# One split of normed rows in the opening of a hybrid encoder layer, with column sums and forget gate from raw rows

## The chip, the cores and the metric

The kernel runs on one core of a Trainium2 chip. The metric is the device time of one execution, in microseconds (us). A core has five engines that run side by side, each through its own instructions in order: TensorE (PE, matrix products; PEld are its weight loads), VectorE (DVE), ScalarE (ACT), GpSimd (POOL) and SyncE (SP, which here issues DMAs). An engine waits for another only through semaphores.

## What is computed

One layer of an encoder trunk for 528 tokens (16 learned meta tokens and 512 of the input) and 1024 channels. The part that matters here, shortened:

```python
h = concatenate([meta, x])                       # 528 x 1024
u = h * rsqrt(mean(h*h) + 1e-6) * norm_mix       # RMSNorm
proj = u @ w_in                                  # projections for everything that follows
# of proj: wd, ad, gd (256 columns), shifted by one token and mixed with mu:
w_log = -softplus(-(w0 + tanh(wd) @ w_lora_up)) - 0.5
a = sigmoid(a0 + ad @ a_lora_up)
g = sigmoid(gd) @ g_lora_up
# of proj: fl, 8 columns, the forget gate of the attention heads
log_f = log_sigmoid(fl + b_f);  F = cumsum(log_f)
# recurrence (RWKV-7) and forgetting attention, gates, output projection,
# second RMSNorm and a squared-ReLU MLP follow
```

## The kernel before

Tokens lie along the free dimension: the input is held transposed, as 8 blocks of 128 channels by 528 tokens, in two halves of 264 tokens (`xt[0]`, `xt[1]`), each loaded in four pieces of two blocks. An fp32 product is replaced by three faster ones: both operands are split into a high and a low part of type fp32r (`uhi`, `ulo` for the input, `whi`, `wlo` for the weights), and high*high, high*low and low*high are added up in PSUM (`passes`). A high part is a cast on ACT, a low part a subtraction on DVE.

The opening (lines 333 to 401) works so. For each half and piece, ACT squares the rows (`sq`, L352). ACT and DVE make `uhi` and `ulo` from rows that are multiplied with the channel gain but not yet normed (L355, L356). PE adds the squares over the channels with a 128x128 matrix of ones in fp32 (`pss`, L360), and computes the 8 forget gate columns as split products (`pf`, L365). ACT makes the scale factor of each token, `rs`, with Ln and Exp (L368, L369). PE multiplies the first weight block (`B_LORA`: `wd` and `ad`) with the half (L304); its result is multiplied with `rs` afterwards (`normed_shift`, L377), then shifted and mixed (`tshift`, L317, L318). After both halves come the forget gate's bias, log-sigmoid and running sum (L381 to L388), tanh and split of the first block (L390, L391), and the second weight block (`B_GD`: `gd`, L393). Meanwhile DVE multiplies the rows with gain and `rs` in place (L398), and ACT and DVE split them a second time, now as normed rows (L400, L401). All later projections read this second split.

The rest of the layer is written as streams that a planner (`Turns`, `Clock`) interleaves by due times; it fixes PE's order by hand (`manual_schedule`), while the order on the other engines is the compiler's. The first things in it are the small products of the decay (`pup`, L720), which read the tanh of the first block (`lhi`, `llo`), and the projection blocks (L501), for which weights are converted at L470 (ACT) and L471 (DVE). The attention reads the forget gate's running sum `fF` through DRAM (L599). SP's queue issues the input's first half, the first weight block, the second half, the second weight block, constants, and then the weights of later blocks as buffers come free.

Of the kernel before, what the change touches and what calls it, by code (L numbers as in the profile page):

```python
# [9 lines left out]
F32 = mybir.dt.float32  # L10
# [9 lines left out]
T = 528  # L20
# [166 lines left out]
def kernel(ctx, tc, ht, x, win, par, cst, gain, lora, wout, wo, wup, wdn, out, dbg=None):  # L187
# [92 lines left out]
    with ExitStack() as st:  # L280
# [3 lines left out]
        opening = ["pj", "pj", "ch", "py"]  # L284

# [10 lines left out]
        def proj(blk, evac, parts=((0, HT), (HT, T)), w=None):  # L296

            w = w or load_w(win[blk], (G, V))
            for a0, a1 in parts:
                po = ppj(opening.pop(0))[:, :a1 - a0]  # L300
                n = 0
                for k in range(KB):
                    for a, b in passes(wk(w, k), U):
                        mm(po, a, b[:, k, a0:a1], start=n == 0, stop=n == 23)  # L304
                        n += 1
                evac(po, slice(a0, a1))

# [3 lines left out]
        def tshift(blk, dst):  # L311

            tm = rp.tile([128, 1 + T], F32, name="tm")
# [13 lines left out]
        fF = rp.tile([8, T], F32, name="fF", tag="lc")  # L327
        fF_d = dr.tile([8, T], F32, name="fF_d")
        f0 = rp.tile([8, T], F32, name="f0", tag="tha")
        f1 = rp.tile([8, T], F32, name="f1", tag="sq")  # L330
        lfs = [rp.tile([128, TP], F32, name=f"lf{i}", tag=("okk", "orr")[i]) for i in range(2)]
        lf, gf = (x[:, :T] for x in lfs)
        with tc.tile_pool(name="xp", bufs=2) as xp:
# [6 lines left out]
            w_lora = load_w(win[B_LORA])  # L340
            for c in range(4):
                nc.sync.dma_start(xt[1][:, 2 * c:2 * c + 2, :].rearrange("p a b -> p (a b)"), ht[1, c])
            w_gd = load_w(win[B_GD])
            nc.sync.dma_start(cs, cst)
            wf = [xp.tile([128, 64], F32R, name=f"wf{i}", bufs=1) for i in range(2)]
            split(wf[0], wf[1], pr[:, C_FL:])
            rss = []
            for t in range(2):
                tk = slice(HT * t, HT * t + HT)
                for c in range(4):  # L350
                    sq = xp.tile([128, 2, HT], F32, name="sq", bufs=3)
                    act(sq, xt[t][:, 2 * c:2 * c + 2, :], AF.Square)  # L352
                    for k in range(2 * c, 2 * c + 2):
                        gn = pr[:, C_GN + k:C_GN + k + 1]
                        act(uhi[:, k, tk], xt[t][:, k, :], AF.Copy, scale=gn)  # L355
                        V.scalar_tensor_tensor(ulo[:, k, tk], xt[t][:, k, :], gn, uhi[:, k, tk].bitcast(F32), ALU.mult, ALU.subtract)  # L356
                    if c == 0:
                        pq = psm("pss")[:, :HT]
                    for k in range(2):
                        mm(pq, ones, sq[:, k, :], start=c + k == 0, stop=c + k == 4)  # L360
# [1025 lines left out]
```

## Time and profile before

| what | us |
|---|---|
| median of 3 runs | 854.1 (852.3 to 855.1) |
| the profiled execution | 852.0 |
| its span, first to last instruction | 850.2 |
| PE busy in the span | 827.5 |
| first L360 product on PE | 5.66 |
| first L304 product (first weight block) | 14.45 |
| first L501 product (planned part) | 34.13 |

The times in the views count from the start of the span. The chain of waits follows the work that ended last backwards from the end; its shares say which engine's work or waits fill the time. A row of a timeline gives start, length, engine, line, operation and, in brackets, the idle time ahead of it and what ended it. The table of groups by form gives for each kind of instruction the number, the busy time, the mean length in ns, and the idle time ahead of it.

### The profile page before, as it was taken

How to read it: one execution, taken by the hardware profiler on the slowest of the kernel's cores; microseconds unless marked ns; L12 is line 12 of the kernel's file. 1: busy time of each engine (PE TensorE's matmuls, PEld its weight loads, DVE VectorE, ACT ScalarE, POOL GpSimd, SP SyncE). 2: the span in 40 equal slices, each digit the busy share in tenths (PEclk: the TensorE clock that was granted, in tenths of full speed). 3: DMA queues.
4: the chain of work that ended last, by engine and by line, in shares of the span. 5: the costliest groups of instructions: out<-in, count | busy, mean ns of one | idle time of the engine just before them, and what ended most of it. 6: DMA issues, size and time to landing. Idle time of an engine off the chain costs nothing.

```text
span 850.2 us, 15285 instructions
## 1 busy us (share of the span) xinstructions
PE 827.5 (97%) x5740; PEld 679.1 (80%) x5740; DVE 618.1 (73%) x1222; ACT 454.0 (53%) x923; POOL 133.5 (16%) x133
## 2 busy tenths in 40 slices
PE   7999989999999999999999999999999999999998
PEld 6888977878887787677788779888888888888886
DVE  6996976679867876566357564877787677768788
ACT  7857536765656337654465442664355435534452
POOL 1041300003012000000012101203700560055000
PEclk9999999999999999999999999999999999999999
DMA  6132231111222212123386432651743274346421
GB/s 225 52 103 59 64 122 43 39 55 36 71 93 82 80 58 89 39 87 100 120 286 221 151 103 75 195 165 50 240 157 99 78 250 132 87 130 192 119 93 74
DMA packets 51338, 95.88 MB, mean 113 GB/s; under 512 B 5816, under 2 KB 6968, under 8 KB 51264
## 3 DMA queue, kind: packets, MB, share of 16 engines
q1 hardware_dynamic: 47680, 86.52, 32.0%
q0 software_dynamic: 1280, 4.20, 1.6%
q10 hardware_dynamic: 2304, 4.20, 1.5%
q8 instruction: 45, 0.74, 0.4%
q14 instruction: 29, 0.24, 0.1%
HBM read 88.57 MB, written 6.31 MB: 112 GB/s over the span
## 4 chain that ended last, share of the span: by engine, by line
PE 78%; DVE 10%; DMA 5%; ACT 3%; issue 3%; POOL 1%; SPq 0%; DVEq 0%; ACTq 0%; POOLq 0%
PE pj L501 24%; PE po L1137 21%; PE po L1255 12%; PE pd L1255 5%; DMA gl<-gd 2%; PE po L1107 2%; PE psc L611 1%; PE pw L845 1%; DVE wlo L471 1%; DMA wraw<-in_wo 1%; PE py L656 1%; PE ppt L640 1%; DVE wlo L236 1%; PE psr L794 1%; PE pch L905 1%
## 5 line engine op out<-in xcount | busy, mean ns | idle before, releaser
L501 PE MATMUL pj<-uhi,whi 128*128 128x264 f32 (+1 forms) x480 | 165.9, 346 | 0.0
L501 PE MATMUL pj<-ulo,whi 128*128 128x264 f32 (+1 forms) x480 | 154.3, 321 | 1.4 <-DVE ulo L401 1.4
L501 PE MATMUL pj<-uhi,wlo 128*128 128x264 f32 (+1 forms) x480 | 154.3, 321 | 0.0
L501 PEld LDWEIGHTS pj<-uhi,whi 128*128 128x128 f32 x480 | 90.3, 188 | 15.0 <-issue 6.7
L236 DVE TENSOR_TENSOR wlo<-wraw,whi 128x512 fp32r<-128x512 f32 x88 | 70.4, 809 | 38.2 <-ACT whi L235 35.9
L501 PEld LDWEIGHTS pj<-ulo,whi 128*128 128x128 f32 x480 | 90.6, 189 | 8.2 <-issue 1.7
L501 PEld LDWEIGHTS pj<-uhi,wlo 128*128 128x128 f32 x480 | 90.4, 188 | 7.2
L1137 PE MATMUL po<-zhi,whi 128*128 128x512 f32 (+1 forms) x248 | 94.8, 382 | 0.0
L1137 PE MATMUL po<-zlo,whi 128*128 128x512 f32 (+1 forms) x248 | 94.8, 382 | 0.0
L1137 PE MATMUL po<-zhi,wlo 128*128 128x512 f32 (+1 forms) x248 | 94.8, 382 | 0.0
L235 ACT CAST whi<-wraw 128x512 fp32r<-128x512 f32 x88 | 53.8, 617 | 51.4 <-DMA wraw<-in_wup 23.3
L471 DVE TENSOR_TENSOR wlo<-wraw,whi 128x512 fp32r<-128x512 f32 x80 | 61.3, 773 | 17.3 <-ACT whi L470 16.9
L470 ACT CAST whi<-wraw 128x512 fp32r<-128x512 f32 x80 | 48.9, 617 | 35.1 <-PE pj L501 33.8
L270 ACT CAST whi<-t 128x512 fp32r<-128x512 f32 x64 | 39.9, 624 | 44.4 <-DVE wlo L271 20.6
L271 DVE TENSOR_TENSOR wlo<-t,whi 128x512 fp32r<-128x512 f32 x64 | 49.3, 782 | 18.9 <-ACT whi L270 18.0
L1255 PE MATMUL po<-wlo,fhi 128*128 128x512 f32 x160 | 62.7, 392 | 0.2 <-DVE wlo L271 0.2
L1255 PE MATMUL po<-whi,flo 128*128 128x512 f32 x160 | 62.3, 390 | 0.0
L1255 PE MATMUL po<-whi,fhi 128*128 128x512 f32 x160 | 61.9, 389 | 0.0
L1183 POOL TENSOR_TENSOR t<-traw 128x512 f32<-128x512 f32 x24 | 34.9, 1462 | 155.1 <-DVE wlo L271 136.0
L1137 PEld LDWEIGHTS po<-zlo,whi 128*128 128x128 f32 x248 | 46.6, 188 | 9.1
L1137 PEld LDWEIGHTS po<-zhi,wlo 128*128 128x128 f32 x248 | 46.6, 188 | 9.0
L1137 PEld LDWEIGHTS po<-zhi,whi 128*128 128x128 f32 x248 | 46.6, 188 | 9.0
(307 smaller groups left out, 1754.8 us busy)
## 6 DMA issues: line engine op xcount, KB each, us to landing
wraw<-in_win SPq DMA_DIRECT2D x84, 256.0 KB, 2.6
wraw<-in_wup SPq DMA_DIRECT2D x64, 256.0 KB, 3.4
wraw<-in_wdn SPq DMA_DIRECT2D x48, 256.0 KB, 2.7
traw<-in_wdn SPq DMA_DIRECT2D x48, 256.0 KB, 3.0
gd<-gt ACTq DMA_DIRECT2D x16, 256.0 KB, 2.2
wraw<-in_wout SPq DMA_DIRECT2D x16, 256.0 KB, 3.1
gl<-gd SPq DMA_DIRECT2D x16, 256.0 KB, 3.2
wraw<-in_wo SPq DMA_DIRECT2D x16, 256.0 KB, 3.5
```

Source lines behind the costliest of these rows:

```text
L235: A.copy(hi, raw)
L236: low.tensor_tensor(lo, raw, hi.bitcast(F32), ALU.subtract)
L270: A.copy(hi, x)
L271: V.tensor_tensor(lo, x, hi.bitcast(F32), ALU.subtract)
L470: A.copy(hi, raw)
L471: low.tensor_tensor(lo, raw, hi.bitcast(F32), ALU.subtract)
L501: mm(po, a, b[:, k, a0:a1], start=n == 0, stop=n == 23)
L611: mm(sc, q[hs, 128 * i:128 * i + 128], k[hs, a:b], start=True, stop=True)
L1107: mm(po, a[:, k, 128 * i:128 * i + 128], b[:, k, :], start=n == 0, stop=n == 23)
L1137: mm(po[:, t0:t1], a, b[:, k, t0:t1], start=n == 0, stop=n == 23)
L1183: eng.tensor_tensor(t, sums[c, pair] if c in (T1, T2) else c, d, ALU.add)
L1255: mm(x[i], a[:, k, left, 128 * i:128 * i + 128], c, start=start and k == 0 and n == 0, stop=stop and k == n_pairs - 1 and n == 2)
```

## The change

The input is split once, as normed rows. The first split, from rows that are not normed, is gone, and so is the normalising of the results in PSUM. Everything on PE that reads the split now comes after `rs`.

- The sums of squares and the forget gate are computed in fp32 from raw rows. Each product fills 32 output columns (`x[32 * g:32 * g + 32]`), and block `g` of four goes to its own group of columns, so that a half's 8 blocks fall into 4 groups twice. The weights of the forget gate are multiplied with the gain and padded from 8 to 32 columns (`wf`). A further product with ones adds the four groups of squares (`root`); for the forget gate a 128x8 matrix `pick` does so, after all projections.
- Both weight blocks are loaded ahead of the second half of the input, and multiplied piece by piece, side by side.
- The opening of PE, ACT, DVE and POOL is written out in the order of the code (`manual_schedule`). Three of the four weight residuals there, and the first two later ones (`low = V if converted else G`), are made by POOL.
- The forget gate's bias, log-sigmoid and running sum become `forget()`, called after the first decay; the attention's tiles wait for it (`yield forgot`). Buffers of `fF`, `f0`, `f1` move to other tags.

```diff
+            def sums(t, c, po):
+                for x, a, b in ((po[1], wf, xt[t][:, chunks[c], :]), (po[0], None, sqs[t, c])):
+                    for k in range(2):
+                        g = 2 * (c % 2) + k
+                        mm(x[32 * g:32 * g + 32], ones[:, :32] if a is None else a[:, 2 * c + k, :], b[:, k, :], start=c < 2, stop=c > 1)
+            def root(t):
+                pq = psm("pss")[:, :HT]
+                mm(pq, ones, part[t][0], start=True, stop=True)
+                act(rss[t], pq, AF.Ln, bias=eps, scale=1.0 / (32 * 1024))
+                act(rss[t], rss[t], AF.Exp, scale=-0.5)
...
+            with tc.manual_schedule(engines={ET.PE, ET.Activation, ET.DVE, ET.Pool}):
...
+                for c in range(4):
+                    square(0, c)
+                    sums(0, c, col[0])
+                V.tensor_copy(part[0][0], col[0][0])
+                high(0)
+                root(0)
+                rest(V, 0)
+                high(2)
+                rest(G, 2)
+                pos = [ppj("pj")[:, :HT] for i in range(2)]
+                scaled(0, 0)
+                upper(0, 0)
+                scaled(0, 1)
+                high(1)
+                rest(G, 1)
+                lower(0, 0)
+                products(0, 0, pos)
...
+                for c in range(4):
+                    sums(1, c, col[1])
+                lower(0, 3)
+                A.copy(part[1][0], col[1][0])
+                root(1)
+                products(0, 3, pos)
...
+                products(1, 3, pos1)
+                V.tensor_reduce(pick, ident.rearrange("p (g a) -> p a g", g=4)[:, :8, :], AX.X, ALU.add)
+                for t in range(2):
+                    pf = psm("pf")[:8, :HT]
+                    mm(pf, pick, part[t][1], start=True, stop=True)
+                    V.tensor_tensor(f0[:, tks[t]], pf, rss[t][:8], ALU.mult)
+                for i in range(2):
+                    shifts[i](pos1[i], tks[1])
+            tanh(lf[:64], lf[:64])
             split(lhi[:, B_LORA, :], llo[:, B_LORA, :], lf)
...
-            low = V
+            low = V if converted else G
...
+                yield forgot
```

The order of the instructions on PE, at the start of the program. Before, where `pss` are the sums of squares and `pf` the forget gate:

```order
L360 MATMUL pss<-sq,ones 128x264 x6
L365 MATMUL pf<-uhi,wf_152 8x264
L365 MATMUL pf<-ulo,wf_152 8x264
L365 MATMUL pf<-uhi,wf_153 8x264
L365 MATMUL pf<-uhi,wf_152 8x264
```

The same place of the changed kernel, up to the first projection product:

```order
L360 MATMUL pf<-xt_116,wf 32x264 x2
L360 MATMUL pss<-sq,ones 32x264 x2
L360 MATMUL pf<-xt_116,wf 32x264 x2
L360 MATMUL pss<-sq,ones 32x264 x2
L360 MATMUL pf<-xt_116,wf 32x264 x2
L360 MATMUL pss<-sq,ones 32x264 x2
L360 MATMUL pf<-xt_116,wf 32x264 x2
L360 MATMUL pss<-sq,ones 32x264 x2
L364 MATMUL pss<-part_150,ones 128x264
L383 MATMUL pj<-uhi,whi 128x264
```

The forget gate's 24 products of a half and the 8 of the ones have become 16 of 32 columns, and one product with ones stands between them and the first projection. On PE at the end of the opening, before (`pup` are the decay's products, `lw` its weights):

```order
L720 MATMUL pup<-lhi,lw_471 128x264 x2
L304 MATMUL pj<-ulo,whi 128x264
L304 MATMUL pj<-uhi,wlo 128x264
L304 MATMUL pj<-uhi,whi 128x264
L304 MATMUL pj<-ulo,whi 128x264
L304 MATMUL pj<-uhi,wlo 128x264
L720 MATMUL pup<-llo,lw_471 128x264 x2
```

and of the changed kernel, behind its last projection product:

```order
L453 MATMUL pf<-part_151,pick 8x264
L453 MATMUL pf<-part_153,pick 8x264
L793 MATMUL pup<-lhi,lw_415 128x264 x2
L793 MATMUL pup<-llo,lw_415 128x264 x2
L793 MATMUL pup<-lhi,lw_416 128x264 x2
L793 MATMUL pup<-lhi,lw_415 128x264 x2
L793 MATMUL pup<-llo,lw_415 128x264 x2
L793 MATMUL pup<-lhi,lw_416 128x264 x2
L558 MATMUL pj<-uhi,whi 128x264
```

Before, products of the second weight block stood between those of the decay; now these follow each other, ahead of the first L558 product (L501 before). ACT's queue at the same place of the changed kernel, where `tm` belongs to the token shift, `f_107` is the forget gate and `lf_109`, `lf_110` are the two blocks:

```order
L303 ACTIVATE tm<-pj,pr 128x264 x2
L527 CAST whi<-wraw 128x512
L586 ACTIVATE f_107<-f_107,pr 8x528
L255 ACT_TABLE_LOAD
L255 ACTIVATE lf_109<-lf_109 64x528
L255 ACTIVATE lf_110<-lf_110 128x528
```

The forget gate's bias stands ahead of the table load, and the tanh of both blocks behind it, ahead of the casts that make `lhi`.

More of the change, by code (lines that the diff above doesn't have):

```diff
@@ new lines, in lower, with products @@
+            def lower(t, c):
+                V.tensor_tensor(ulo[:, chunks[c], tks[t]], xt[t][:, chunks[c], :], uhi[:, chunks[c], tks[t]].bitcast(F32), ALU.subtract)
+            def products(t, c, pos):
+                for x, po in enumerate(pos):
+                    for k in range(2 * c, 2 * c + 2):
+                        i = 2 * x + k // 4
+                        for n, (a, b) in enumerate(passes((whi[i], wlo[i]), U)):
+                            mm(po, a[:, 128 * (k % 4):128 * (k % 4) + 128], b[:, k, tks[t]], start=k + n == 0, stop=k == 7 and n == 2)
```

158 lines of the change are left out of this document (86 added, 72 removed).

## The prediction

> **What bounds the kernel now.** I read the page first: the span, the busy shares and the chain that ended last.
>
> ```profile
> span 850.2 us, 15285 instructions
> PE 827.5 (97%) x5740; PEld 679.1 (80%) x5740; DVE 618.1 (73%) x1222; ACT 454.0 (53%) x923; POOL 133.5 (16%) x133
> PE 78%; DVE 10%; DMA 5%; ACT 3%; issue 3%; POOL 1%; SPq 0%; DVEq 0%; ACTq 0%; POOLq 0%
> ```
>
> PE is idle for only 22.7 of 850.2 us, and the change leaves PE's order from the first L501 product on as it was. So what counts is when PE gets there. Next, the table of windows over the opening and what follows it (columns: length, PE, PEld, DVE, ACT, POOL busy, PE clock, DMA share, GB/s).
>
> ```profile
> 5.66:34.13 28.47, 28.46 (x189) 24.30 (x189) 25.38 (x56) 23.35 (x48) 0.28 (x2) 1.00 0.45 153
> 34.13:58.27 24.14, 22.75 (x185) 21.29 (x184) 22.57 (x40) 18.02 (x35) 8.69 (x9) 1.00 0.28 89
> 58.27:72.00 13.73, 11.77 (x108) 8.39 (x107) 12.19 (x22) 7.49 (x14) 0.97 (x2) 1.00 0.17 59
> 276.40:280.00 3.60, 3.60 (x43) 2.52 (x38) 1.67 (x3) 0.72 (x2) 0.00 (x0) 0.53 0.07 26
> ```
>
> In the opening PE never stops (28.46 of 28.47), although DVE and ACT are nearly full too (25.4 and 23.4). PE's timeline gives the landmarks.
>
> ```profile
> 5.66 5.18 PE L360 MATMUL pss<-sq,ones 128*128 128x264 f32 x12 [5.66 <-ACT sq L352]
> 14.45 0.28 PE L304 MATMUL pj<-uhi,whi 128*128 128x264 f32 x1
> 17.35 3.72 PE L360 MATMUL pss<-sq,ones 128*128 128x264 f32 x16
> 20.71 0.48 PE L365 MATMUL pf<-uhi,wf 128*8 128x264 f32 x1
> 23.80 0.29 PE L304 MATMUL pj<-uhi,whi 128*128 128x264 f32 x1
> 34.13 0.39 PE L501 MATMUL pj<-uhi,whi 128*128 128x264 f32 x1
> 38.86 0.39 PE L501 MATMUL pj<-ulo,whi 128*128 128x264 f32 x1 [1.39 <-DVE ulo L401]
> ```
>
> The first L501 product starts at 34.13, and soon stops 1.39 for the second split of the input, which the change does away with. The point to beat is therefore 34.13 + 1.39 = **35.5**.
>
> **What PE loses and gains.** An fp32 product over 264 columns is two records. In the first row twelve take 5.18 (0.43 each), in the third sixteen 3.72 (0.23): PE is at half speed up to about 10 us, though the windows give a clock of 1.00 there; the spacing decides. Removed per half: the ones products, 20.71 - 17.35 = 3.36, and 24 forget-gate products, 23.80 - 20.71 = 3.09; together 12.9 for both halves. Added: 32 products of 32 columns, and four fp32 products of 0.45 (two of ones, two of pick). No row shows a 128x32 tile. The nearest, from the groups by form:
>
> ```profile
> L656 PE MATMUL py<-pT,vt 128*64 128x512 f32 x16 | 4.3, 618 | 0.0
> L777 PE MATMUL pbn<-sq,rkb 128*128 128x512 f32 x8 | 4.2, 606 | 0.5 <-ACT sg L255 0.5
> ```
>
> Sixteen records of half width cover 4.3 us, eight of full width 4.2: two column groups run side by side. With four groups and the order forget, forget, square, square per piece I count five rounds per half, 5 x 0.45 = 2.2 (ends: 16 x 0.45 = 7.1 one after another, 1.8 in four full rounds). I take 2.2. PE then streams 12.9 - 4.4 - 1.8 = 6.7 less. That is a gain only if PE is not kept waiting. The first split of the input (L355, L356) and the normalising of the results (L377) go too; PE waited for neither in 5.66:34.13, so beyond the 1.39 they are costed at nothing.
>
> **What it waits for.** Before, PE multiplied unnormed rows while the scale factor was made. Now no projection starts before it. The rows for the layout (start, length):
>
> ```profile
> 3.67 0.43 SPq L339 DMA_DIRECT2D xt<-in_ht  x1
> DMA to landing us min/median/max: 3.3/5.3/5.9
> 4.96 0.64 ACT L352 ACTIVATE sq<-xt 128x528 f32<-128x528 f32 x1 [1.65 <-DMA xt<-in_ht]
> 12.48 0.48 ACT L368 ACTIVATE rs<-pss,eps 128x264 f32<-128x264 f32 x1 [0.25 <-PE pss L360]
> 13.27 0.41 ACT L369 ACTIVATE rs<-rs 128x264 f32<-128x264 f32 x1
> 20.18 4.11 DVE L398 SCALAR_TENSOR_TENSOR xt<-xt,pr,rs 128x264 f32<-128x264 f32 x10
> 32.38 1.69 ACT L400 CAST uhi<-xt 128x528 fp32r<-128x528 f32 x3
> 33.95 1.31 DVE L401 TENSOR_TENSOR ulo<-xt,uhi 128x528 fp32r<-128x528 f32 x2
> ```
>
> *First scale factor.* The fourth piece of the input lands between 3.67 + 3.3 and 3.67 + 5.9; I take 8.2, near the middle. Forget products of that piece to 9.1, square sums at half speed to 10.3, copy 0.4, ones product 0.6, Ln 0.48, Exp 0.41 and hops: **12.4**.
>
> *First half.* Scaling is 0.41 a row-block, the lower part 0.61 a piece: 8 x 0.41 + 4 x 0.61 = 5.7 on DVE, with the cast (0.56) between. PE needs 1.45 per piece (12 x 0.12: the 24 products from 14.45 to 17.35 take 2.9), so DVE leads: the third lower part is ready at 17.6, if POOL doesn't interfere, and three pieces are multiplied at 19.0. Second half's sums 2.2 with their ends, copy 0.5, ones product 0.6, Ln and Exp: second scale factor at 23.6.
>
> *Second half.* DVE does the same 5.7 and two token shifts of 0.41; each lower part also waits for the cast of its own piece, which the in-order queue can't fill, some 2.2 in all. 23.6 + 5.7 + 0.8 + 2.2 = 32.3, and the last piece is multiplied at 33.8.
>
> *Tail.* Before, the tanh of the LoRA block, its split and the table load lay beside the second block's products:
>
> ```profile
> 24.67 0.74 ACT L381 ACTIVATE f<-f,pr 8x528 f32<-8x528 f32 x1 [2.62 <-DVE f L371]
> 29.10 1.28 ACT L390 ACT_TABLE_LOAD   x1
> 30.40 0.64 ACT L390 ACTIVATE lf<-lf 64x528 f32<-64x528 f32 x1
> 31.47 0.63 ACT L270 CAST lhi<-lf 128x528 fp32r<-128x528 f32 x1
> 32.15 0.39 PE L720 MATMUL pup<-lhi,lw 64*128 64x264 f32 x2
> 32.59 0.69 DVE L271 TENSOR_TENSOR llo<-lf,lhi 128x528 fp32r<-128x528 f32 x1
> ```
>
> Now both blocks end together, and pup stands ahead of every L501 product with nothing between. After the last product: pick products 0.9, two small DVE products 0.8, the forget bias 0.7 (ahead of the table load in ACT's queue), load 1.3, two tanh 1.2 (both ahead of the cast), cast 0.6, lower part 0.7, rest of pup 0.7, less small overlaps: **6.4**, of which PE works 2.3. L501 starts at 33.8 + 6.4 = 40.2, against 35.5: **+4.7**. All the waits together are more than the 6.7 saved.
>
> *POOL.* Five weight residuals move from DVE to POOL. DVE and POOL, where both read two tensors of SBUF:
>
> ```profile
> 51.46 1.76 POOL L759 TENSOR_TENSOR KT<-BK,P 64x576 f32<-64x576 f32 x1
> 52.10 1.73 DVE L768 TENSOR_TENSOR L<-orr,P 128x576 f32<-128x576 f32 x1
> 53.30 1.69 POOL L770 TENSOR_TENSOR sq<-orr,sg 128x512 f32<-128x512 f32 x1
> 53.75 1.78 DVE L471 TENSOR_TENSOR wlo<-wraw,whi 128x512 fp32r<-128x512 f32 x1
> 61.73 0.67 DVE L471 TENSOR_TENSOR wlo<-wraw,whi 128x512 fp32r<-128x512 f32 x1
> L1183 POOL TENSOR_TENSOR t<-traw 128x512 f32<-128x512 f32 x24 | 34.9, 1462 | 155.1 <-DVE wlo L271 136.0
> ```
>
> The same DVE instruction takes 0.67 alone and 1.78 beside POOL, and both slow ones end 0.5 to 0.6 after the POOL instruction beside them (51.46 + 1.76 = 53.22 against 53.83, 54.99 against 55.53): they take turns. Three residuals of about 1.4 fall among the first half's scaling, where DVE leads, and two in the second half. Laid out with turns, L501 starts at 45.2: **+9.7**. Ends +4.7 (all hidden) and +9.7; I take **+7.5**, nearer the upper because the rows show the turns each time, and below it because a residual that falls into a wait of DVE is free.
>
> *Costed at nothing.* wf's memset and product are done before the first piece lands. The second half of the input lands about 2 us later, two weight pieces of 256 KB being ahead of it in SP's queue, but its squares come only at 16; if not, up to 2. Pick's reduce has no row of its kind; between 0.1 and 0.7, it ends before the last product. The forget chain (Exp, Ln, scan) now stands in ACT's and DVE's queues ahead of the first key block's evacuation: up to +1 there; against it DVE has six lower parts of 0.61 fewer after 34, which may give back some of the 1.96 that PE idles in 58.27:72. I take 0, with ends -2 and +1. Its result is first read by the attention, long after.
>
> **Sum.** The profiled execution took 852.0 us around its span of 850.2; + 7.5 = 859.5. It lies 2.1 under the median of 854.1, so the median I forecast is **861.5**.
>
> **The clock.** The last row of windows shows a mean of 0.53 over 3.6 us, which is 3.4 us at half speed, behind waits of PE of under 1 us near 274. No such drop follows the longest inner wait:
>
> ```profile
> L611 PE MATMUL psc<-ka,qa 64*128 64x144 f32 x16 | 2.6, 335 | 2.4 <-DVE AX L851 2.4
> ```
>
> So the rows neither tie the drop to the length of a wait nor exclude it behind the new ones, which are longer. The Trainium skill, "TensorE: Matmul & The Clock Gate", section "HAM oscillation — how this bites in real kernels", warns of idle gaps over some 3.4 us, after which PE runs at half clock again. This rule speaks against the change, whose tail leaves PE idle for about 4 us. By it rival (b) is what happens, and the median would be 863 to 865. No wait inside this trace is that long, so the trace can't confirm it; the drop at 276 came without one.
>
> **Rivals.** (a) *No turns lost*: POOL's residuals fall into DVE's waits, +4.7 and 0 to -2 later: 858. For it: POOL is nearly idle in the opening; against: the doubled rows. (b) *Half clock behind the new waits*: 3.4 us at half speed lose 1.7 behind the tail, and up to as much in the first half, so 861.5 + 1.7 to 3.4, say 864. For it: 0.53 near 276; against: 2.4 idle without a drop. (c) *The change does not do what it says*: the column groups run one after another. Then 2 x (7.1 - 2.2) = 9.8 more, part at half speed: 871. Against it: the L656 row. (d) *PE's work decides, and the kernel gets faster*: 6.7 less streaming and the 1.39 stall gone are 8.1, so 846 for the median at best; I put 848, with 2 of waits left. Its place is the two scale factors and the tail. It decides once the new waits of PE up to L501 stay under 10 us together; my layout has 15 even without POOL's turns: 40.2, less 4.96 when the first piece is there, less 20.2 of work (sums 4.4 and 1.0 more at half speed, 96 projection products 11.6, the four 1.8, pup 1.4). For it: PE was 100% busy in the opening; against it: every wait above is a chain of single instructions on in-order queues.
>
> **How the numbers follow.** Forecast 0.50 (861.5, its own range 858 to 865); (a) 0.20; (b) 0.10; (c) 0.07; (d) 0.13. Leaving out (c) and (d), 0.20, the range spans the others with their bounds. Below: 854.1 + 4.7 - 2, less 1.2 if the fourth piece lands at 7.0. Above: 854.1 + 9.7 + 1 + 1.7. With the 1.4 by which single runs stray from their middle (852.3 to 855.1) on either side this is **854 to 868**. About 0.3% (2.6 us) is what a measurement of this kernel can tell from no change. Faster: (d), 0.13. Same: a quarter of (a) and a little of the forecast, 0.09. Slower: 0.78.
>
> **What would show it.** Right: in the changed profile the first L558 product starts between 40 and 46; PE idles some 4 us behind the pick products, waiting for lhi; the first L383 product waits for scaled rows after 12; DVE's scaling beside POOL's residual takes 1.5 to 1.8 instead of 0.48; the 32-column products come in groups of two to four. Wrong: L558 before 35.5, or the 128x32 rows spaced 0.45 apart one by one, or gains past 72 us, where PE's work and order are unchanged.

## The result, and the profile after

The changed kernel takes **864.4 us** (median of 4 runs, 863.56 to 866.95), the kernel before 854.0 beside it: ratio **1.0137**, 95% interval 1.0118 to 1.0155. It is 1.4% slower. (The ratio, here and below, is formed from the single runs and not from the two medians; their quotient, 1.0122, lies inside the interval.) Its profiled execution took 864.99 us. These are the page's span, the busy shares and the shares of the chain that ended last, of the changed kernel:

```profile
span 863.2 us, 15240 instructions
PE 829.6 (96%) x5732; PEld 678.1 (79%) x5732; DVE 611.5 (71%) x1200; ACT 449.6 (52%) x909; POOL 140.7 (16%) x138
PE 80%; DVE 5%; DMA 5%; ACT 3%; issue 2%; POOL 0%; SPq 0%; DVEq 0%; ACTq 0%; POOLq 0%
```

The span grew by 13.0 us. PE's idle time grew from 22.7 to 33.6 us, and its busy time did not fall although it has less to stream, since some of it ran at half speed, as the rows below show. Where did the 13 us go? The first product of the recurrence (`psr`) is a landmark well behind the opening. PE's timeline (start, length) of the kernel before:

```profile
55.50 0.89 PE L794 MATMUL psr<-L,BK 64*64 64x128 f32 x24
```

And PE's timeline of the changed kernel, landmarks only:

```profile
10.37 1.25 PE L364 MATMUL pss<-part,ones 128*128 128x264 f32 x2 [0.54 <-DVE part L394]
14.24 0.59 PE L383 MATMUL pj<-uhi,whi 128*128 128x264 f32 x1 [2.62 <-ACT uhi L373]
17.02 0.59 PE L383 MATMUL pj<-ulo,whi 128*128 128x264 f32 x1 [2.19 <-DVE ulo L376]
...
20.48 0.42 PE L383 MATMUL pj<-ulo,whi 128*128 128x264 f32 x1
20.70 0.43 PE L383 MATMUL pj<-uhi,wlo 128*128 128x264 f32 x1
...
21.33 0.28 PE L383 MATMUL pj<-uhi,whi 128*128 128x264 f32 x1
21.45 0.28 PE L383 MATMUL pj<-ulo,whi 128*128 128x264 f32 x1
...
23.23 0.67 PE L360 MATMUL pf<-xt,wf 128*32 128x264 f32 x8
...
24.59 1.16 PE L360 MATMUL pss<-sq,ones 128*32 128x264 f32 x8
26.23 0.71 PE L364 MATMUL pss<-part,ones 128*128 128x264 f32 x2 [0.48 <-ACT part L426]
...
29.56 0.39 PE L383 MATMUL pj<-uhi,whi 128*128 128x264 f32 x1 [1.18 <-ACT uhi L373]
...
38.04 0.39 PE L383 MATMUL pj<-ulo,whi 128*128 128x264 f32 x1 [1.22 <-DVE ulo L376]
...
39.58 1.06 PE L453 MATMUL pf<-part,pick 128*8 128x264 f32 x4
44.93 0.59 PE L793 MATMUL pup<-lhi,lw 64*128 64x264 f32 x2 [4.29 <-ACT lhi L270]
...
47.07 0.59 PE L558 MATMUL pj<-uhi,whi 128*128 128x264 f32 x1
...
68.43 0.89 PE L867 MATMUL psr<-L,BK 64*64 64x128 f32 x24
```

From `psr` to the end of the span are 850.2 - 55.50 = 794.7 us before and 863.2 - 68.43 = 794.8 after. The whole loss, 12.9 us, lies ahead of `psr`, and 11.6 of it already at the first block product (47.07 against 34.13 + 1.39). In the brackets the reader sees what replaced a PE that never stopped: 2.62 and 2.19 us for the first scaled rows, 0.38 to 1.22 four times around the second half (three are shown), 4.29 for the high part of tanh.

The rows show a second thing. Up to 20.93 PE's products stand 0.22 us apart, from 21.09 on 0.12: the 18 steps from 17.02 to 21.09 take 4.07 us, where 18 x 0.12 is 2.2. So PE is at half speed here, for about 1.9 us more, although the windows give a clock of 1.00; as in the prediction's first row the spacing decides. In the kernel before, products stood 0.12 apart from 14.45 on.

DVE's timeline of the changed kernel shows the turns with POOL. A row with "x4" groups four equal instructions in a row:

```profile
12.62 3.72 DVE L370 SCALAR_TENSOR_TENSOR xt<-xt,pr,rs 128x264 f32<-128x264 f32 x4 [1.71 <-ACT rs L366]
16.27 0.69 DVE L376 TENSOR_TENSOR ulo<-xt,uhi 128x528 fp32r<-128x528 f32 x1
...
17.70 1.78 DVE L376 TENSOR_TENSOR ulo<-xt,uhi 128x528 fp32r<-128x528 f32 x1
...
27.95 1.71 DVE L370 SCALAR_TENSOR_TENSOR xt<-xt,pr,rs 128x264 f32<-128x264 f32 x4 [6.25 <-ACT rs L366]
...
36.33 1.66 DVE L376 TENSOR_TENSOR ulo<-xt,uhi 128x528 fp32r<-128x528 f32 x1 [1.30 <-ACT uhi L373]
```

And POOL's, of the same stretch:

```profile
13.18 2.88 POOL L349 TENSOR_TENSOR wlo<-wraw,whi 128x512 fp32r<-128x512 f32 x2 [9.45 <-ACT whi L346]
17.61 1.30 POOL L349 TENSOR_TENSOR wlo<-wraw,whi 128x512 fp32r<-128x512 f32 x1 [1.55 <-ACT whi L346]
34.69 2.73 POOL L528 TENSOR_TENSOR wlo<-wraw,whi 128x512 fp32r<-128x512 f32 x2 [15.78 <-ACT whi L527]
```

Four scaled rows take 3.72 us beside POOL and 1.71 without it, a lower part 1.78 or 1.66 beside POOL and 0.69 without: 2.0 + 1.1 + 1.0 = **4.1 us** of DVE. ACT's timeline shows the tail:

```profile
41.13 0.73 ACT L586 ACTIVATE f<-f,pr 8x528 f32<-8x528 f32 x1 [0.38 <-DVE f L454]
41.89 1.28 ACT L255 ACT_TABLE_LOAD   x1
43.18 1.18 ACT L255 ACTIVATE lf<-lf 64x528 f32<-64x528 f32 x2
44.26 1.23 ACT L270 CAST lhi<-lf 128x528 fp32r<-128x528 f32 x2
```

Last, windows over the opening (columns as in the prediction; PE, PEld, DVE, ACT, POOL busy, clock): the stretch from 17 to 43 us in the kernel before, then the same stretch and two shorter ones in the changed kernel:

```profile
17.00:43.00 26.00, 24.60 (x186) 22.22 (x184) 25.36 (x56) 20.53 (x43) 0.28 (x2) 1.00 0.21 64
```

```profile
17.00:43.00 26.00, 20.29 (x133) 16.83 (x133) 15.98 (x29) 14.07 (x27) 4.03 (x3) 0.93 0.16 51
31.20:34.70 3.50, 3.42 (x17) 3.12 (x16) 3.04 (x8) 1.64 (x3) 0.01 (x1) 0.51 0.00 0
44.90:51.70 6.80, 6.61 (x33) 6.08 (x34) 4.25 (x8) 5.47 (x11) 0.28 (x2) 0.50 0.03 11
```

DVE, which was busy for 25.36 of these 26.00 us before, is busy for 15.98 now: the change does take work from it here, but its instructions wait for one another. And the clock is one half in two places: behind the second half's waits of 1.18 and 0.38, and behind the 4.29 of the tail.

### The profile page after: what moved, and what is told of

Same layout as the page of the kernel before. It is cut to its first block, busy times and chain, and to the rows that moved or that the text cites. A ratio compares the mean times of both kernels' runs of the same rounds, so it can differ in the third digit from the quotient of the medians.

```text
span 863.2 us, 15240 instructions
## 1 busy us (share of the span) xinstructions
PE 829.6 (96%) x5732; PEld 678.1 (79%) x5732; DVE 611.5 (71%) x1200; ACT 449.6 (52%) x909; POOL 140.7 (16%) x138
## 4 chain that ended last, share of the span: by engine, by line
PE 80%; DVE 5%; DMA 5%; ACT 3%; issue 2%; POOL 0%; SPq 0%; DVEq 0%; ACTq 0%; POOLq 0%
PE pj L558 26%; PE po L1211 20%; PE po L1329 12%; PE pd L1329 5%; DMA gl<-gd 2%; PE po L1181 2%; PE pw L918 1%; PE psc L684 1%; DMA wraw<-in_wo 1%; PE py L729 1%; DVE wlo L236 1%; PE ppt L713 1%; PE psr L867 1%; PE pssq L625 1%; DMA wraw<-in_wup 1%
## 5 line engine op out<-in xcount | busy, mean ns | idle before, releaser
L558 PE MATMUL pj<-uhi,whi 128*128 128x264 f32 (+1 forms) x480 | 167.2, 348 | 0.0
L558 PE MATMUL pj<-ulo,whi 128*128 128x264 f32 (+1 forms) x480 | 155.3, 324 | 0.0
L558 PE MATMUL pj<-uhi,wlo 128*128 128x264 f32 (+1 forms) x480 | 155.1, 323 | 0.0
L558 PEld LDWEIGHTS pj<-uhi,whi 128*128 128x128 f32 x480 | 91.5, 191 | 15.2 <-issue 6.9
L558 PEld LDWEIGHTS pj<-uhi,wlo 128*128 128x128 f32 x480 | 91.6, 191 | 7.0
L558 PEld LDWEIGHTS pj<-ulo,whi 128*128 128x128 f32 x480 | 91.7, 191 | 6.6 <-issue 1.7
L236 DVE TENSOR_TENSOR wlo<-wraw,whi 128x512 fp32r<-128x512 f32 x84 | 68.0, 819 | 37.5 <-ACT whi L235 35.3
L235 ACT CAST whi<-wraw 128x512 fp32r<-128x512 f32 x84 | 51.3, 617 | 51.8 <-DMA wraw<-in_wup 25.0
L528 DVE TENSOR_TENSOR wlo<-wraw,whi 128x512 fp32r<-128x512 f32 x78 | 59.5, 767 | 20.5 <-ACT whi L527 20.1
L527 ACT CAST whi<-wraw 128x512 fp32r<-128x512 f32 x80 | 49.2, 618 | 42.1 <-PE pj L558 36.6
```

Source lines behind the costliest of these rows:

```text
L235: A.copy(hi, raw)
L236: low.tensor_tensor(lo, raw, hi.bitcast(F32), ALU.subtract)
L527: A.copy(hi, raw)
L528: low.tensor_tensor(lo, raw, hi.bitcast(F32), ALU.subtract)
```

## The experiments

Theories: **T1**, the turns of DVE and POOL; **T2**, the waits for the scale factors and for tanh; **T3**, the half clock behind the waits. Rivals: **D**, PE's streaming alone sets the opening; **S**, the split of the normed rows on DVE and ACT is a second bound. Each run was timed beside the kernel before; only ratios to it are compared. First block product and `psr` are starts in one profiled execution of each kernel.

| kernel | ratio (95%) | first block product | psr |
|---|---|---|---|
| before | 1 | 34.13 | 55.50 |
| change | 1.0137 (1.0118 to 1.0155) | 47.07 | 68.43 |
| e1_no_pool | 1.0123 (1.0106 to 1.0139) | 44.29 | 65.34 |
| e2_blocks_first | 1.0101 (1.0085 to 1.0117) | 39.76 | 65.35 |
| e3_tail_first | 1.0125 (1.0109 to 1.0141) | 42.78 | 64.53 |
| e7_orders | 1.0055 (1.0035 to 1.0074) | 37.54 | 64.18 |
| e6_warm | 1.0130 (1.0109 to 1.0150) | 43.92 | 65.34 |
| e8_orders_warm | 1.0081 (1.0059 to 1.0103) | 36.97 | 63.62 |
| e10_no_scale_wait | 1.0031 (1.0014 to 1.0047) | 34.12 | 59.69 |
| e11_sums_early | 1.0048 (1.0033 to 1.0063) | 35.90 | 61.47 |
| e12_sums_early2 | 1.0040 (1.0022 to 1.0057) | 35.38 | 61.97 |
| e4_sums_alone | 1.0071 (1.0056 to 1.0086) | 30.89 | 64.30 |
| e5_sums_alone2 | 1.0002 (0.9987 to 1.0017) | 31.15 | 58.19 |
| e9_late_forget | 0.9996 (0.9978 to 1.0014) | 29.50 | 56.97 |

The column `psr` is not the whole time. From `psr` to the end are 791.2 (e5) to 796.2 us (e1), 794.7 before. In e2 and in the kernels built on e7, 170 or 171 of PE's instructions stand between the first block product and `psr`, in the others 152 to 154; the rest of that spread is not explained by these runs.

### The orders: e1, e2, e3, and e7 with all three

**e1_no_pool** (the places of the three residuals among DVE's passes shift by one or two):

```diff
-                rest(G, 2)
+                rest(V, 2)
-                rest(G, 1)
+                rest(V, 1)
-                rest(G, 3)
+                rest(V, 3)
-            low = V if converted else G
+            low = V
```

> All five residuals that the change gave to POOL go to DVE (the LoRA and GD weights' three and both of the first projection block); nothing else is changed. The program's opening no longer has a POOL residual beside a DVE pass. Theory T1 (the two engines take turns, and that is on the path): DVE's first four scaled rows fall from 3.72 us to about 1.7, the two parts of 1.78 and 1.66 us to 0.70, DVE takes 5 x 0.7 us more of its own, and the first product of the projection blocks comes at 44 to 46 us instead of 47.07: time 861 to 863 where the changed kernel has 864.4. Theory T2 (the waits for the two scale factors and for tanh are what costs, the turns lie beside them): first block product at 46.5 to 49, time 864 to 866.

Measured 1.0123, 0.14% under the change, which is 1.2 us with an uncertainty of 2.1. DVE's timeline of e1:

```profile
12.05 1.71 DVE L370 SCALAR_TENSOR_TENSOR xt<-xt,pr,rs 128x264 f32<-128x264 f32 x4 [1.71 <-ACT rs L366]
13.68 0.68 DVE L349 TENSOR_TENSOR wlo<-wraw,whi 128x512 fp32r<-128x512 f32 x1
```

The scaled rows are back at 1.71 and the first block product comes at 44.29, as T1 expected. But the time moved by less than the uncertainty: on POOL the residuals cost DVE 4.1 us, on DVE five (one of them late) cost 0.68 each. Taking turns is real; that giving the work back to DVE is any faster is not shown.

**e2_blocks_first** (`gone` is set behind the first 24 block products; `x_` is the block product, `picked` the last product of L453, so that none moves ahead of the pick):

```diff
+                                if done == n == 0:
+                                    after(x_, picked)
...
                 lw = load_lora(p, 0, 1)
+                if p == 0:
+                    yield gone
```

> The changed kernel with TensorE's order turned at one place: the first 24 products of the first projection block (L558) stand ahead of the LoRA up-products that wait for tanh, right behind the pick. Theory T2 (TensorE's 4.29 us of waiting for tanh's high parts is on the path): the first block product comes at 40.3 to 41 us instead of 47.07, the up-products wait under 1 us, and the time falls by 3.5 to 5.5 us, to 859 to 861. If the wait only covers another one (the recurrence waits for the decay rates anyway), the time stays within 1 us of 864.4. Theory T3 (half clock behind that wait costs on top): the products from 40 to 47 us stand 0.12 us apart rather than 0.22, and the gain is over 5 us.

Measured 1.0101: 0.36% or 3.1 us under the change (uncertainty 2.1). PE's timeline of e2:

```profile
39.76 0.39 PE L558 MATMUL pj<-uhi,whi 128*128 128x264 f32 x1
...
44.13 0.39 PE L798 MATMUL pup<-lhi,lw 64*128 64x264 f32 x2 [1.19 <-ACT lhi L270]
```

The wait for tanh is 1.19 instead of 4.29, so the tail was on the path. T2 holds here; the gain lies just under the expected 3.5 to 5.5, well within the uncertainty. The wait was expected under 1 us.

**e3_tail_first**:

```diff
                 products(1, 3, pos1)
+                shifts[0](pos1[0], tks[1])
+                tanh(lf[:64], lf[:64])
+                split(lhi[:, B_LORA, :], llo[:, B_LORA, :], lf)
+                shifts[1](pos1[1], tks[1])
...
-                for i in range(2):
-                    shifts[i](pos1[i], tks[1])
```

> The changed kernel with the tail in another order: the second half's LoRA shift, tanh and its split stand ahead of the pick's forget-gate products on DVE and ACT, and the pick's own reduce stands earlier, so the forget bias no longer runs before tanh on ACT. Theory T2: the up-products start at 41.5 to 43 us instead of 44.93, TensorE's wait for them falls from 4.29 us to 1.3 to 2.8, and the time falls by 1.5 to 3.5 us, to 861 to 863. If another engine sets the end of the opening (T1 alone), the time stays within 0.7 us of 864.4.

Measured 1.0125, 1.1 us under the change (uncertainty 2.1): not told apart from nothing. The up-products wait 2.43 instead of 4.29, as expected, and start at 40.41, earlier than the expected 41.5 to 43; the time gained is a little below the 1.5 to 3.5 that T2 gave, and 0 is not excluded.

**e7_orders**:

> The three edits of e1_no_pool, e2_blocks_first and e3_tail_first together in the changed kernel. Alone they gave ratios to before of 1.0123, 1.0101 and 1.0125 where the change has 1.0137. If the three waits add up: 1.0137 - 0.0014 - 0.0036 - 0.0012 = 1.0075, some 6.4 us over the kernel before. If e2 and e3 take the same wait away twice: 1.0085 to 1.0095. The rest that stays (about 6 us) is then the two scale factors and the half clock behind them.

Measured **1.0055**: 0.82%, 7.0 us under the change (uncertainty 2.3). The three add up (0.14 + 0.36 + 0.12 = 0.62) within the uncertainty. So over half of the loss is the order in which the change lays out its opening, with the engine that makes the residuals, and not what it computes. The rest, 0.55%, is met below.

### The clock: e6 and e8

**e6_warm** (`idle` is a free PSUM bank; the calls for 12, 3 and 10 products are left out here):

```diff
+            def warm(po, n, cols):
+                for i in range(n):
+                    mm(po[:, :cols], ones, part[0][0][:, :cols], start=True, stop=True)
...
                 pos = [ppj("pj")[:, :HT] for i in range(2)]
+                idle = ppj("ch")
+                warm(idle, 14, 64)
...
+                warm(psm("idle"), 9, HT)
```

> The changed kernel with fp32 products that nobody reads put into TensorE's waits of the opening: 14 of 64 columns behind the first scale factor's sum, 12 behind the first product on normed rows, 3 and 10 around the second scale factor, 9 of 264 columns behind the pick. Nothing else is changed. Theory T3 (the clock falls to one half behind each wait of some 3 us, and the products behind it run at half speed): the granted clock stays at 1.0 from about 12 to 60 us, the products from 17 to 21 us and from 47 to 52 us stand 0.12 us apart instead of 0.22, and the time falls by 3 to 6 us (ratio to before 1.007 to 1.010 instead of 1.0137). T1 and T2 alone: the time stays within 1 us (1.0125 to 1.015), since the waits for DVE and ACT set the opening anyway.

**e8_orders_warm** is e7 with the same products at all places but the last.

> e7_orders with the unread products of e6_warm in the first three places (the tail's wait holds block products already). Theory T3: 2 to 4 us below e7_orders, ratio to before about 1.004 to 1.006. Without a cost of the half clock ahead of 35 us: the same as e7_orders. If TensorE's 6.7 us less work were all that is left once the waits are covered, it would come to 0.995 to 1.0.

Measured 1.0130 (0.6 us under the change, uncertainty 2.4) and 1.0081 (2.2 us *over* e7, uncertainty 2.5). Windows of e7, then of e8:

```profile
10.00:40.00 30.00, 24.00 (x156) 19.89 (x157) 17.89 (x38) 17.55 (x33) 0.00 (x0) 0.83 0.32 113
```

```profile
10.00:40.00 30.00, 28.68 (x238) 25.77 (x238) 18.73 (x39) 17.89 (x33) 0.00 (x0) 1.00 0.33 114
```

The clock rose from 0.83 to 1.00, yet the first block product came only 0.6 us earlier (36.97 against 37.54): products at full speed reach the next wait for DVE sooner. In e6 the first block product came 3.2 us earlier than in the change, in the profiled execution, which at 861.84 was the fastest of its six (the others 863.0 to 865.0). Behind it, where the change runs at half clock until 51.7, e6 gains nothing: PE's timeline of e6 has a new wait,

```profile
54.79 1.16 PE L825 MATMUL pkk<-sq,cs 128*128 128x264 f32 x4 [1.86 <-ACT sq L821]
```

and from first block product to `psr` are 65.34 - 43.92 = 21.4 us, as in the change (68.43 - 47.07 = 21.4). T3 falls as a cost of 3 us or more; one of 1 or 2 us can be neither shown nor excluded by these runs. What the unread products cost by themselves was not measured either.

### PE's work alone: e4, e5, e9

**e4_sums_alone** takes the kernel before and replaces its ones products and forget gate by the change's column groups:

```diff
-                        mm(pq, ones, sq[:, k, :], start=c + k == 0, stop=c + k == 4)
+                    for cg, a, b in ((col[1], wf, xt[t][:, 2 * c:2 * c + 2, :]), (col[0], None, sq)):
+                        for k in range(2):
+                            g = 2 * (c % 2) + k
+                            mm(cg[32 * g:32 * g + 32], ones[:, :32] if a is None else a[:, 2 * c + k, :], b[:, k, :], start=c < 2, stop=c > 1)
...
-                    for a, b in passes([x[:, 8 * k:8 * k + 8] for x in wf], U):
-                        mm(pf, a, b[:, k, tk], start=n == 0, stop=n == 23)
+                mm(pq, ones, part[0], start=True, stop=True)
+                mm(pf, pick, part[1], start=True, stop=True)
```

> The kernel before with one part of the change alone: squares' column sums and the forget gate in groups of 32 columns in fp32 from raw rows, and the small products that add up the groups. LoRA and GD still multiply unnormed rows, and the normed rows are still split later. Rival D (TensorE's work sets the opening): TensorE streams 6.7 us less, its first product on normed rows comes near 29 us instead of 35.5, time 847 to 849. Theory S (the normed rows' split on DVE and ACT is a second bound close behind): that first product comes at 33 to 35 us, behind a wait for a split part, time 851 to 854. The full change at 864.4 then owes its loss to the normed rows standing ahead of the products, and none of it to the column groups.

Neither came: 1.0071, slower. PE's timeline of e4 tells why:

```profile
31.12 0.28 PE L507 MATMUL pj<-ulo,whi 128*128 128x264 f32 x1
42.48 0.59 PE L507 MATMUL pj<-uhi,wlo 128*128 128x264 f32 x1 [11.08 <-DVE wlo L477]
```

PE was ready 3 us earlier and then stood 11 us for a weight residual that the scheduler had put behind other passes of DVE until 41.76. The run says nothing for or against D; e5 puts that residual ahead.

**e5_sums_alone2**:

```diff
+                with tc.high_priority() if len(converted) < 2 else nullcontext():
                     A.copy(hi, raw)
                     low.tensor_tensor(lo, raw, hi.bitcast(F32), ALU.subtract)
...
-            act(lf[:64], lf[:64], AF.Tanh)
+            after(act(lf[:64], lf[:64], AF.Tanh), logged)
```

> The run e4_sums_alone again, with the residual of the first projection block's weights put ahead on ACT and DVE (in e4 it came at 42 us, and TensorE stood 11.3 us for it behind its first product), and tanh behind the forget gate's logarithm, which saves two table loads. Rival D (TensorE's work alone sets the opening): first product on normed rows at 28 to 30 us without a wait of over 1 us behind it, and 0.7% below the kernel before (ratio 0.991 to 0.995). Theory S (the split of the normed rows on DVE and ACT is a second bound close behind TensorE): the products of the first block wait 3 us or more in sum for lower parts, and the ratio is 0.998 to 1.006.

Measured **1.0002** (0.9987 to 1.0017), in S's range and outside D's. PE's timeline of e5:

```profile
33.42 0.39 PE L508 MATMUL pj<-uhi,whi 128*128 128x264 f32 x1 [0.54 <-ACT uhi L406]
34.76 0.39 PE L508 MATMUL pj<-ulo,whi 128*128 128x264 f32 x1 [0.95 <-DVE ulo L407]
36.84 0.59 PE L508 MATMUL pj<-uhi,whi 128*128 128x264 f32 x1 [1.21 <-ACT uhi L406]
```

The first block starts 3 us earlier (31.15) and its products then wait 3.4 us in six places (three are shown), 1.8 of it for upper parts from ACT and 1.6 for lower parts from DVE; S had named lower parts alone. From 36.4 to 43.3 the granted clock is 0.51 as well. PE's saved work is worth nothing by itself; how much of it goes to the waits and how much to the half clock was not separated.

**e9_late_forget** adds the change's place of the forget gate to e5:

```diff
-            act(f0, f0, AF.Identity, bias=pr[:8, C_BF:C_BF + 1])
...
-            V.tensor_tensor_scan(fF, f0, f1, 0.0, ALU.mult, ALU.subtract)
...
             yield from pairs[0].decay()
+            forget()
```

> The run e5_sums_alone2 (kernel before with the column sums in groups) with one more part of the change: the forget gate's bias, exponential, logarithm and scan stand behind the first decay, as in the changed kernel, and tanh no longer waits for them. That takes 3.1 us of DVE passes on 8 rows out of the stretch in which the normed rows are split. In e5 the first block stood 0.7 + 1.1 + 1.4 us for lower parts and fell to half clock from 36.4 to 43.3 us. Theory S (DVE's work ahead of those parts is the second bound): these waits fall below 1.5 us in sum, the first block's 48th product comes at 38 to 41 us instead of 44.7, and the ratio to before falls from 1.0002 to 0.992 to 0.997, which would be the gain in TensorE work that the change gave away. If S is wrong (the wait is ACT's, or the late forget gate stalls the recurrence behind), the ratio stays at 0.998 to 1.004.

Measured 0.9996 (0.9978 to 1.0014): the expected gain did not come. PE's timeline of e9, and a window over it:

```profile
34.13 0.39 PE L499 MATMUL pj<-ulo,whi 128*128 128x264 f32 x1 [1.78 <-DVE ulo L398]
37.55 0.59 PE L499 MATMUL pj<-uhi,whi 128*128 128x264 f32 x1 [2.54 <-ACT uhi L397]
```

```profile
17.00:43.00 26.00, 21.00 (x148) 17.56 (x140) 24.93 (x54) 22.43 (x44) 0.14 (x1) 0.87 0.12 41
```

ACT's timeline of e9 shows what stands ahead of the upper part behind the longer wait:

```profile
35.04 1.28 ACT L262 ACT_TABLE_LOAD   x1
```

DVE is busy for 24.93 of 26.00 us, and on it the 3.1 us of forget passes were replaced by other passes (the second half's scaled rows, the decay's scan) ahead of the same parts. ACT works without a gap from 32.65 to there: the table load, and behind it the late forget gate's exponential (36.33), stand ahead of the upper part, which starts at 36.88. So the longer wait is ACT's, which is the other case of the expectation. DVE and ACT together are the second bound that S describes; that these 3.1 us of DVE were its price was wrong. The half clock, which e9 has from 36 to 43 us as e5 does, is not ruled out as a part of the cost.

### The scale factors: e10, e11, e12

**e10_no_scale_wait**, from e7, leaves the scale factor out of the rows (`unit` is a tile of ones), so its output is not the layer's; it only shows what the waits for the factor are worth. Some of the scaled rows and one upper part of each half also move ahead; the lines below do not show that:

```diff
-                    V.scalar_tensor_tensor(xt[t][:, k, :], xt[t][:, k, :], pr[:, C_GN + k:C_GN + k + 1], rss[t], ALU.mult, ALU.mult)
+                    V.scalar_tensor_tensor(xt[t][:, k, :], xt[t][:, k, :], pr[:, C_GN + k:C_GN + k + 1], unit, ALU.mult, ALU.mult)
```

> The run e7_orders with the rows multiplied by the gain and by a tile of ones instead of the scale factor, so that nothing waits for the scale factor; the scaling by it is left out of the rows (the forget gate keeps it). The first half's first two scaled pieces stand ahead of the sum's copy, the second half's ahead of the second logarithm. Theory T2 (what is left of the loss in e7, ratio 1.0055, is the two waits for the scale factor, 2.8 + 0.9 and 1.3 + 0.5 us of TensorE standing): the first product on scaled rows comes at 10 to 11.5 us instead of 13.2, the first block product at 33 to 35 instead of 37.5, ratio 0.999 to 1.001. If DVE's passes set the opening whatever the scale factor does: first block product at 36.5 or later, ratio 1.004 to 1.006.

Measured 1.0031 (1.0014 to 1.0047), between the two expectations: 0.24% under e7 (uncertainty 0.26%). The first block product came at 34.12, as T2 said, 3.4 us earlier, yet the kernel is still slower than before, whose own first block product stands at 34.13. PE's timeline of e10 shows what it still waits for:

```profile
13.62 0.59 PE L383 MATMUL pj<-ulo,whi 128*128 128x264 f32 x1 [2.76 <-DVE ulo L376]
...
48.73 1.16 PE L821 MATMUL pkk<-sq,cs 128*128 128x264 f32 x4 [2.20 <-ACT sq L817]
```

The first product came at 10.4 us, as expected, but the second then waited 2.76 for a lower part. And the up-products, which stood ahead of the first block before (32.15), now stand behind 24 of its products, at 37.23; `psr` follows at 59.69 instead of 55.50. The wait of 2.20 for the keys' squares stands behind the opening. It is 2.20 or 2.21 in e7, e8, e10, e11 and e12 alike, and neither the kernel before nor the change has it. No run takes it away, so whether it is what keeps these kernels behind is open.

**e11_sums_early**, from e7, keeps the scale factor and moves the second half's sums ahead:

```diff
                 products(0, 0, pos)
+                square(1, 0)
+                square(1, 1)
...
+                for c in range(4):
+                    sums(1, c, col[1])
+                A.copy(part[1][0], col[1][0])
                 products(0, 1, pos)
```

> The run e7_orders with the second half's squares and column sums moved ahead: they stand behind the first of the four pieces of the first half's products (12 products) instead of the third, and its logarithm and exponential behind the second piece. The scale factor of the second half is then there before the first half's products end, and DVE, which stood from 21.7 to 27.9 us in the changed kernel, goes on to the second half's rows. Theory T2 (the second scale factor's wait, 1.3 + 0.5 us of TensorE and 6 us of DVE, is on the path): second half's scaled rows from 22 to 23 us, first block product at 31 to 34 us instead of 37.5, ratio to before 0.998 to 1.002 instead of 1.0055. If ACT, which now squares ahead of the first half's upper parts, sets the opening: first block product at 36 us or later, ratio 1.004 to 1.007.

Measured 1.0048 at a first block product of 35.90: the ratio of the second expectation, and its place but for 0.1 us. In its trace DVE stood from 19.0 to 24.0 us, for a square that lacked a tile and an upper part queued behind the second logarithm.

**e12_sums_early2** mends both (`bufs=4` for `sq`; `upper(0, 3)` ahead of the sums):

> The run e11_sums_early with two waits mended that its trace showed: the last square of the second half stood 3.2 us for one of three tiles (now four), and the first half's last upper part stood on ACT behind the second logarithm, so that DVE stood from 19.0 to 24.0 us. Theory T2: the second half's scaled rows start at 21 to 22.5 us instead of 24.6, the first block product comes at 32 to 34 us instead of 35.9, and the ratio to before falls from 1.0048 to 1.000 to 1.003. If the place of the first block product no longer decides (the products ahead of the up-products only move the wait to the keys' sums, 2.4 us in e7 and e11), the ratio stays at 1.004 to 1.006.

Measured 1.0040 (1.0022 to 1.0057), 0.15% under e7 (uncertainty 0.26%). PE's timeline of e12, then ACT's:

```profile
17.52 1.12 PE L360 MATMUL pf<-xt,wf 128*32 128x264 f32 x8
18.40 1.12 PE L360 MATMUL pss<-sq,ones 128*32 128x264 f32 x8
```

```profile
21.17 0.38 ACT L422 COPY part<-pss 128x264 f32<-128x264 f32 x1 [2.85 <-PE pss L360]
23.15 0.48 ACT L365 ACTIVATE rs<-pss,eps 128x264 f32<-128x264 f32 x1 [1.60 <-PE pss L364]
```

The second scale factor now waits for PE. The rounds of the column sums stand 0.88 us apart, where the change has some 0.45 (23.23 to 24.59 for three): PE, behind its first waits, runs them at half speed. The scaled rows start at 24.1, not at 21 to 22.5, and the first block product comes at 35.38, not 32 to 34: the expectation of T2 failed. No run beats the kernel before; e5 and e9 equal it.

## Why the prediction was right

It forecast a slower kernel at 861.5 us in a range of 854 to 868; it is 864.4. The mechanism was the one forecast: PE stands at the new waits for longer than the shorter sums save. The sum was too small by 4.1 us at the first block product (35.5 + 7.5 = 43.0 against 47.07), so the prediction's own sign, a first L558 product between 40 and 46, was missed by 1.1; and the measured time is the one that it gave to rival (b), 863 to 865. By its steps:

- **PE streams 6.7 us less.** The column groups run side by side as worked out: rounds of the second half's sums start 0.45 us apart. They run from 23.23 to 25.75, 2.5 us, since the last one stands behind the last square. But e5 shows that this saving alone is worth nothing (ratio 1.0002). The forecast's sum did not need it as a gain; rival (d) rested on it, and fails already without the waits for the scale factors and the late tanh.
- **First scale factor at 12.4.** The scaled rows start at 12.62.
- **The two halves.** Three pieces multiplied at 19.0, second scale factor at 23.6, last piece at 33.8, all without turns; measured 23.2, 27.95 (scaled rows) and 39.6. So the first half took 4 us longer than laid out and the second 1.4.
- **Turns, +7.5 taken.** The value lay between the ends 4.7 and 9.7 on the ground that a residual falling into a wait of DVE is free. The rows of 3.72, 1.78 and 1.66 show DVE's passes lengthened by 4.1 us. PE waits behind the first (2.19) and the third (1.22), but behind the 1.78 it multiplies without a wait from 17.02 to 25.75. That leaves 3.0 us on PE's way, and 4.7 + 3.0 = 7.7 is near the 7.5 taken (an estimate from these rows).
- **Tail 6.4.** From the last piece to the first block product are 47.07 - 39.6 = 7.5 us, with the forget bias, the table load and both tanh ahead of the cast, as forecast; PE waits 4.29, "some 4 us" in the prediction. e2 and e7 show that the tail is on the path.
- **The clock, costed at nothing in the forecast, rival (b).** This is the term that was mis-sized, as far as the profiles show. PE runs at half speed up to 20.93 (by the spacing, 1.9 us more), again behind the second half's waits and behind the tail (windows 0.51 and 0.50). The Trainium skill, "TensorE: Matmul & The Clock Gate", section "What's actually happening", says that the clock falls to one half after an idle window of about 3.4 us: the trace agrees with it behind the tail (4.29 us of waiting, then 6.8 us at 0.50), and not behind the second half's waits, which are shorter. From the first scaled rows to the first block product the change takes 47.07 - 12.62 = 34.5 us, e6, at full clock, 43.92 - 11.94 = 32.0, and e1, without turns, 44.29 - 12.05 = 32.2. So in these profiles the half clock is worth 2.5 us there, over half of what the sum lacked and within rival (b)'s 1.7 to 3.4. It is less where the order is another: from e7 to e8 the same stretch goes from 26.0 to 25.1. And e6 and e8 were not measurably faster, and no more was e1. How much of the 2.5 us is device time stays open, though e12 shows the half speed setting the second scale factor once the sums stand ahead.
- **The stall of 1.39 goes.** It does; but from first block product to `psr` are 21.4 us both before and after. The products that run at half clock until 51.7 take its place, and where they don't (e6), a wait of 1.86 for the keys' squares does.
- **Offset of the median.** The forecast put the median 2.1 above the profiled execution, as before. After, the profiled execution (864.99) lies 0.6 over its median. Profiled against profiled (859.5 against 864.99) the miss is 5.5 us instead of 2.9; that the median came nearer is luck.
- **Unchanged behind 72 us.** 794.7 against 794.8 us from `psr` to the end.

The change's own order costs about 7 of its 12 us (e7). What keeps even the best versions of the change (e10, e12) behind the kernel before is in part argued. Before, PE multiplied unnormed rows while sums, logarithm and scaling ran beside it, and tanh ran beside the second block's products; the change gives up this cover. But e10, in which no row waits for a scale factor, gains 0.24% with an uncertainty of 0.26% and stays 0.31% behind, so the cover of the scale factors is not shown to be the rest. The half clock and the wait of 2.2 us for the keys' squares are left beside it.

## What to carry to other kernels

Work taken from an engine that is 97% busy can be worth nothing if the next engines have little room, as in e5: look at the busy time of the others in that same stretch (25.36 of 26.00 us on DVE here) before counting the saving. Doing a step once instead of twice can cost more than the second time did, if the second time stood beside work that now has to wait for the first. And where an opening is laid out anew, put the longest chain (here shift, table load, tanh, split) ahead of small steps in every in-order queue and independent products behind it; that order was worth more here than the products saved.

## What the hardware showed besides

- *The clock falls behind shorter waits too, but not behind each of them.* In e7 a wait of 2.21 us for the keys' squares (52.14) is followed by half clock; in e6 one of 1.86 at nearly the same place is not. The length alone does not decide: of the same wait in five kernels, those of e7, e8 and e12 are followed by half clock, and those of e10 (48.73) and e11 (50.50) by 1.00. Windows of e7, then of e6:

```profile
53.30:56.70 3.40, 3.40 (x17) 3.40 (x17) 3.40 (x8) 1.69 (x3) 1.54 (x1) 0.50 0.49 155
```

```profile
53.30:56.70 3.40, 1.91 (x12) 1.78 (x13) 3.06 (x8) 1.23 (x3) 1.37 (x1) 1.00 0.53 159
```

The stretches at one half last 3.4 or 6.8 us in most of these profiles, and some 13.7 in e4, where they begin about 3.5 us into its wait of 11.08.
- *DVE and POOL.* Without POOL's residuals four scaled rows take 1.71 us, beside them 3.72. The Trainium skill, "SBUF — State Buffer", section "SBUF: two separate sides", describes an exclusive lock that one of the two holds for a whole instruction; both rows agree with that, and e1 adds the price: beside the residuals DVE's passes took 4.1 us longer, against 0.68 for each residual when DVE does it itself.
